# A gated causal convolution inside Strassen products: the weights, instead of the activations, stream through TensorE

## The chip, the cores and the metric

The kernel runs on one core of a Trainium2 chip. TensorE (PE) multiplies: it holds a 128x128 block of one operand (the stationary one, loaded by its own instruction, PEld) and streams columns of the other through it (the moving one) into a PSUM bank. VectorE (DVE) and ScalarE (ACT) work on tiles, GpSimd (POOL) here mainly issues DMAs, SyncE (SP) issues the other DMAs. The metric is the device time of one execution in microseconds (us), as the median of several runs.

## The reference

One hybrid block on 512 positions of width 1024: a normalised input is projected by a wide `w_in`; one branch is a short gated convolution, the other a chunked mLSTM; both are projected back and merged by gates, followed by two smaller projections. The part that matters here is the convolution branch, in float32:

```python
hn = rmsnorm(x, g_mix[l])
proj = jnp.einsum('bsd,de->bse', hn, w_in[l])
(xa, ba, ca, za, q, k, v, o, zb, ig, fg, ga, gb) = jnp.split(proj, SPLIT_POINTS, axis=-1)
# y[s] = w[0] u[s-2] + w[1] u[s-1] + w[2] u[s], with u = 0 before the start
ya = ba * causal_short_conv(ca * xa, conv_w[l], conv_b[l])
ya = jnp.einsum('bsc,cd->bsd', ya * jax.nn.silu(za), w_a_out[l])
```

`silu(z)` is z * sigmoid(z). `xa`, `ba`, `ca` and `za` are 512 x 1024 each. The convolution runs along the positions, separately for each channel, and `w_a_out` then contracts over the channels.

## The kernel before, in words

Every float32 product is made of three TensorE matmuls on a high and a low part (`mm3`, L234 to L236: high x high, low x high, high x low). The parts of the activations (`hn_hi`, `hn_lo`, and sums of them in `hs`) are made early; those of the weights are made as the weights arrive. A weight operand is a tile of 4 blocks of 128 rows by 512 columns (`wraw`); `split_half` makes its parts in two halves of 128x1024 elements: the high part `whi` on ACT (L181), the low part `wlo` on DVE (L182). Each has two buffers.

The order on PE, ACT, DVE and POOL is the order in which the program is written (a manual schedule), and each engine works strictly in it. After each stretch of matmuls the program calls `step`, and `step` calls `tick`, which writes down the work of the other engines for this stretch, in this order: the new tasks that the stretch before left in `fresh` (snaps of PSUM banks and what follows), one `split_half` of the operand that comes next, and then one more piece of every task in `active` and of those begun earlier (a task is a generator; a `yield` ends its piece).

Four times, for the channels 128c to 128c + 255 with c = 0, 2, 4, 6 (a pair of 128-channel blocks each, called first to fourth pair below), `strassen` computes one 512 x 1024 piece of the projection, the 256 columns each of x, c, b and z, as seven products instead of eight. Product j uses weight operand j; some operands are sums of two blocks of weights, made in place by accumulating DMAs that POOL issues (L157), or by DVE (L186). A product has two steps i = 0, 1, so a pair has 14 ticks, and the two halves of the next operand are split at the two ticks of the product before. The tasks `t1` to `t6` snap the banks into `s` and `v` (L347, on ACT) and add or subtract them (`out`, L351, on DVE). The four finished quarters go to `sink(n, t, ...)`: n = 0 is the x and c part, n = 1 the b and z part.

Before, the pairs run with the last argument of `strassen` true: the weights are stationary and 256 positions of activations move, so that the results come out with channels on the partitions and positions along them, one half of the positions at a time. `sink_conv` sorts its quarters to `first` to `fourth`: product of x and c into `cu`, three taps for each channel block into `cv`, gate by b, z and its sigmoid `cz`, and `put` writes the high part of the result to one tile named `ya` on ACT (L409) and the low part to another on DVE (L411). The block behind the pairs multiplies by `w_a_out` and reads `ya` as its moving operand, 512 positions wide.

Much later, in the tail, `lefts_3` prepares operands of a last set of Strassen products; `cut` (L241 on ACT, L242 on DVE) makes the high and low part of one of them, a tile named `ls`.

Of the kernel before, what the change touches and what calls it, by code (L numbers as in the profile page):

```python
# [9 lines left out]
F32 = mybir.dt.float32  # L10
# [4 lines left out]
P = 128  # L15
# [21 lines left out]
def hybrid_block(ctx, tc, x, p, g_mix, w_in, conv_w, conv_b, w_a_out, b_gates, g_head,  # L37
# [352 lines left out]
    def sink_conv(c, u, v, ya, ct):  # L390
# [4 lines left out]
        part = [slice(f * H2, (f + 1) * H2) for f in range(2)]  # L395
        held = {}

        def taps(f):
            to = v[:, part[f]]
            dve.tensor_scalar(to, u[:, f, 2:], w[f][2], None, ALU.mult)  # L400
            for j in range(2):
                dve.scalar_tensor_tensor(to, u[:, f, j:j + H2], w[f][j], to, ALU.mult, ALU.add)

        def put(src, h):
            if not ya:
                ya.extend(hp.tile([P, KT, S], F32R, name=f"ya{i}", tag=t, align_bytes=256) for i, t in enumerate(("qk", "vv")))
            to = [t[:, c:c + 2, h * H2:(h + 1) * H2] for t in ya]
            src = src.rearrange("p (f s) -> p f s", f=2)
            act.activation(to[0], src, AF.Copy)  # L409
            yield  # L410
            dve.tensor_tensor(to[1], src, to[0].bitcast(F32), ALU.subtract)  # L411

        def split(t):
            return t.rearrange("p (f s) -> p f s", f=2)

        def first(i, src):
            if i == 0:
                held["x"] = src
                return
            dve.memset(u[:, :, :2], 0.0)  # L420
            dve.tensor_tensor(u[:, :, 2:], split(held["x"]), split(src), ALU.mult)
            for f in range(2):
                yield
                taps(f)

        def second(i, src):
            if i == 0:
                for f in range(2):
                    dve.scalar_tensor_tensor(v[:, part[f]], v[:, part[f]], b[f], src[:, part[f]], ALU.add, ALU.mult)
                return  # L430
            z = temp("e", "cz")
            act.activation(z, src, AF.Sigmoid)
            dve.tensor_tensor(v, v, src, ALU.mult)
            yield
            dve.tensor_tensor(v, v, z, ALU.mult)
            yield
            yield from put(v, 0)

        def third(i, src):
            if i == 0:  # L440
                held["b"] = src
                return
            z = temp("e", "cz")
            act.activation(z, src, AF.Sigmoid)
            g = held["g"] = ct[0]
            dve.tensor_tensor(g, held["b"], src, ALU.mult)
            yield
            dve.tensor_tensor(g, g, z, ALU.mult)

        def fourth(i, src):  # L450
            if i == 0:
                held["x"] = ct[1]
                act.activation(held["x"], src, AF.Copy)
                yield
                return
            dve.tensor_copy(u[:, :, :2], u[:, :, H2:])
            dve.tensor_tensor(u[:, :, 2:], split(held["x"]), split(src), ALU.mult)
            g = held["g"]
            for f in range(2):
                yield  # L460
                taps(f)
            yield
            for f in range(2):
                dve.scalar_tensor_tensor(g[:, part[f]], v[:, part[f]], b[f], g[:, part[f]], ALU.add, ALU.mult)
            yield
            yield from put(g, 1)

        def sink(n, t, src):
            yield from ((first, fourth), (second, third))[n][t // 2](t % 2, src)
# [1074 lines left out]
```

## Time and profile before

| | us |
|---|---|
| median of 3 runs | 838.02 |
| lowest, highest run | 837.71, 838.5 |
| the profiled execution | 837.85 |
| its span in the profile | 836.1 |
| PE busy | 826.2 |
| DVE busy | 681.8 |
| ACT busy | 531.1 |
| POOL busy | 210.3 |

The span is the stretch that the trace covers, and 1.75 us of the execution lie around it. Busy times overlap, so each is read against the span, not added up. In the rows of a timeline stand start, duration, engine, line, operation, the tile written, an arrow, and the tiles read; in brackets the engine's idle time ahead of the row, and what ended it. PE's durations include its pipeline, so that consecutive matmuls overlap, and the time that one costs is the distance between starts. In the rows of windows stands, for each engine, its busy time and the number of instructions.

### The profile page before, as it was taken

The page shows a single profiled execution, that of the slowest core. Times are in us where ns is not written, and L with a number is a line of the kernel's source. Part 1 is how long each engine was busy: PE and PEld are TensorE (multiplying, and loading weights), DVE is VectorE, ACT ScalarE, POOL GpSimd, SP SyncE. Part 2 cuts the span into 40 slices and gives each one's busy share as a digit, 9 for nine tenths or more (in the row PEclk, how much of TensorE's full clock was granted, in tenths as well). Part 3 has the DMA queues.
Part 4 walks back from the last instruction along what each step waited for, and adds up shares of the span by engine and source line. Part 5 has one row for each costly group of instructions (what it writes and reads, how often), then busy time and mean ns, then how long its engine had stood idle before and what let it go on. Part 6 is the DMA issues. An engine that isn't in the chain of part 4 may idle for free.

```text
span 836.1 us, 12130 instructions
## 1 busy us (share of the span) xinstructions
PE 826.2 (99%) x4521; PEld 720.9 (86%) x4521; DVE 681.8 (82%) x944; ACT 531.1 (64%) x790; POOL 210.3 (25%) x212
## 2 busy tenths in 40 slices
PE   9999999999999999999999999999999999999995
PEld 7888888888889988888888999999998888888885
DVE  6688768998888777889878999797885779999565
ACT  6567665778665866577876484545448357757643
POOL 4203122213125221320322434242410212121031
PEclk9999999999999999999999999999999999999999
DMA  9748789769869897995997789999989698799402
GB/s 314 270 149 183 151 222 221 206 205 264 212 142 190 223 228 176 255 214 154 263 233 187 154 179 235 181 181 182 185 271 378 135 250 205 191 270 238 170 1 101
DMA packets 102947, 170.74 MB, mean 204 GB/s; under 512 B 5664, under 2 KB 47700, under 8 KB 102120
## 3 DMA queue, kind: packets, MB, share of 16 engines
q0 software_dynamic: 39136, 69.28, 44.0%
q1 hardware_dynamic: 59968, 94.64, 34.5%
q10 hardware_dynamic: 3784, 6.04, 2.2%
q8 instruction: 35, 0.57, 0.3%
q14 instruction: 24, 0.20, 0.1%
HBM read 153.16 MB, written 16.79 MB: 203 GB/s over the span
## 4 chain that ended last, share of the span: by engine, by line
PE 93%; DVE 5%; issue 1%; ACT 1%; POOLq 0%; POOL 0%; ACTq 0%; DVEq 0%
PE mm L235 28%; PE mm L234 28%; PE mm L236 28%; DVE wlo L182 2%; PE pv L234 1%; PE pv L236 1%; PE pv L235 1%; PE mm L590 1%; PE mmp L590 1%; PE sc L236 1%; PE sc L235 1%; PE sc L234 1%; PE ptp L491 0%; PE ptk L1329 0%; DVE xr L1353 0%
## 5 line engine op out<-in xcount | busy, mean ns | idle before, releaser
L182 DVE TENSOR_TENSOR wlo<-wraw,whi 128x1024 fp32r<-128x1024 f32 x245 | 300.7, 1228 | 81.3 <-ACT whi L181 75.0
L181 ACT ACTIVATE whi<-wraw 128x1024 fp32r<-128x1024 f32 x246 | 257.9, 1054 | 80.2 <-PE mm L236 38.0
L157 POOL DMA_DIRECT2D wraw<-in_w_in x106 | 129.3, 1390 | 296.0 <-DVE wlo L182 212.3
L347 ACT ACTIVATE s<-mm 128x512 f32<-128x512 f32 x84 | 50.2, 598 | 78.4 <-PE mm L236 77.2
L235 PE MATMUL mm<-wlo,hs 128*128 128x512 f32 x256 | 99.8, 390 | 0.0
L234 PE MATMUL mm<-whi,hs 128*128 128x512 f32 x256 | 99.7, 389 | 0.0
L236 PE MATMUL mm<-whi,hs 128*128 128x512 f32 x256 | 99.7, 389 | 0.0
L234 PE MATMUL mm<-hn_hi,whi 128*128 128x256 f32 (+1 forms) x304 | 93.3, 307 | 0.0
L236 PE MATMUL mm<-hn_hi,wlo 128*128 128x256 f32 (+1 forms) x304 | 93.0, 306 | 0.0
L235 PE MATMUL mm<-hn_lo,whi 128*128 128x256 f32 (+1 forms) x304 | 92.9, 305 | 0.0
L234 PE MATMUL mm<-hs,whi 128*128 128x256 f32 x320 | 90.6, 283 | 0.0
L235 PE MATMUL mm<-hs,whi 128*128 128x256 f32 x320 | 90.6, 283 | 0.0
L236 PE MATMUL mm<-hs,wlo 128*128 128x256 f32 x320 | 90.6, 283 | 0.0
L234 PE MATMUL mm<-whi,hn_hi 128*128 128x512 f32 x192 | 74.7, 389 | 0.0
L235 PE MATMUL mm<-wlo,hn_hi 128*128 128x512 f32 x192 | 74.7, 389 | 0.0
L236 PE MATMUL mm<-whi,hn_lo 128*128 128x512 f32 x192 | 74.7, 389 | 0.0
L234 PEld LDWEIGHTS mm<-hs,whi 128*128 128x128 f32 x320 | 61.4, 192 | 0.0
L235 PEld LDWEIGHTS mm<-hs,whi 128*128 128x128 f32 x320 | 61.4, 192 | 0.0
L236 PEld LDWEIGHTS mm<-hs,wlo 128*128 128x128 f32 x320 | 61.4, 192 | 0.0
L234 PEld LDWEIGHTS mm<-hn_hi,whi 128*128 128x128 f32 x304 | 58.1, 191 | 2.8 <-DVE hn_lo L245 0.4
L236 PEld LDWEIGHTS mm<-hn_hi,wlo 128*128 128x128 f32 x304 | 58.1, 191 | 2.6
L235 PEld LDWEIGHTS mm<-hn_lo,whi 128*128 128x128 f32 x304 | 58.1, 191 | 2.4
(342 smaller groups left out, 1724.6 us busy)
## 6 DMA issues: line engine op xcount, KB each, us to landing
wraw<-in_w_in SPq DMA_DIRECT2D x32, 1024.0 KB, 6.0
wraw<-in_w_in SPq DMA_DIRECT2D x46, 512.0 KB, 5.0
wraw<-in_w_in POOLq DMA_DIRECT2D x46, 512.0 KB, 7.4
wraw<-in_w_in POOLq DMA_DIRECT2D x60, 256.0 KB, 5.9
wraw<-in_w_b_out SPq DMA_DIRECT2D x7, 1024.0 KB, 6.9
wraw<-in_w_b_out POOLq DMA_DIRECT2D x12, 512.0 KB, 6.8
wraw<-in_w_o SPq DMA_DIRECT2D x5, 1024.0 KB, 6.2
wraw<-in_w_a_out SPq DMA_DIRECT2D x4, 1024.0 KB, 5.1
```

The source lines that it names most:

```text
L157: nc.gpsimd.dma_start(raws[to][:, ks, cs], src[:, ks, :], accum_op=ALU.add)
L181: act.activation(hi, t, AF.Copy)
L182: (e_lo or dve).tensor_tensor(lo, t, hi.bitcast(F32), ALU.subtract)
L234: pe.matmul(ps, lhsT=a[0], rhs=b[0], start=first, stop=False, **kw)
L235: pe.matmul(ps, lhsT=a[0], rhs=b[1], start=False, stop=False, **kw)
L236: pe.matmul(ps, lhsT=a[1], rhs=b[0], start=False, stop=last, **kw)
L347: act.activation(to[i], src, AF.Copy, scale=scale)
L590: pe.matmul(pss[n, t], lhsT=pT[u][:, k, t * P:(t + 1) * P], rhs=(whi, wlo)[v][2 * n + k], start=(k, i) == (0, 0), stop=(k, i) == (1, 2))
```

## The change

The four pairs now run with activations stationary (a block of 128 channels of the input by 128 positions) and the 512 columns of a weight operand moving, as other products of this kernel do: 24 matmuls of 512 columns a product in place of 48 of 256. The results then have positions on the partitions and channels along them, while the convolution and the next product need channels on the partitions. So:

- x * c is written to `u`, a quarter of `m` (L461). PE transposes it by 8 matmuls with the identity (`turned`, L403) into two PSUM banks `ptu`; ACT copies them with the last tap's weight and the bias (L426), and DVE adds the two other taps from PSUM (L409, `taps`).
- b and z go to a new tile `zb` (`place`), where b * z * sigmoid(z) is made (L468 to L471). For the first three pairs DVE transposes it in blocks of 32x32 (L474) and ACT moves the blocks into place in 16 instructions on 32 partitions each (L445), two in a tick. For the last pair PE transposes `zb`, by 8 more matmuls right behind those for `u`.
- `gated` multiplies both on DVE (L412) and writes the high part of `ya` on ACT (L413); `rest` writes the low part on DVE (L416).
- All this is the task `after`, which runs in the ticks of the next pair, starting one tick in (two after the first pair); the last pair's runs in the block of `w_a_out`.
- In the tail, the two parts of `ls` are made a step apart: the low part one step later than before.

```diff
@@ -387,86 +387,91 @@
         product(6, acc, None, lambda i: sink(0, 2 + i, acc[i]))
         order.reverse()
 
-    def sink_conv(c, u, v, ya, ct):
+    def sink_conv(c, zb, ya, last):
 
 
         w = [[cw[:, j * KT + c + f:j * KT + c + f + 1] for j in range(3)] for f in range(2)]
         b = [cb[:, c + f:c + f + 1] for f in range(2)]
-        part = [slice(f * H2, (f + 1) * H2) for f in range(2)]
-        held = {}
-
-        def taps(f):
-            to = v[:, part[f]]
-            dve.tensor_scalar(to, u[:, f, 2:], w[f][2], None, ALU.mult)
-            for j in range(2):
-                dve.scalar_tensor_tensor(to, u[:, f, j:j + H2], w[f][j], to, ALU.mult, ALU.add)
-
-        def put(src, h):
+        u, blocks = (m[:, i, :].rearrange("p (t f) -> p t f", t=NT) for i in (2, 3))
+        g, v = (m[:, i, :].rearrange("p (f s) -> p f s", f=2) for i in range(2))
+        gs = [g[:, f, :] for f in range(2)]
+
+        def turned(src):
+            pts = [ps_x.tile([P, S], F32, name="ptu", tag="x") for _ in range(2)]
+            for f in range(2):
+                for t in range(NT):
+                    pe.transpose(pts[f][:, t * P:(t + 1) * P], src[:, t, f * P:(f + 1) * P], ident)
+            return pts
+
+        def taps(f, pt):
+            for j in (1, 0):
+                to = v[:, f, 2 - j:]
+                dve.scalar_tensor_tensor(to, pt[:, :S - 2 + j], w[f][j], to, ALU.mult, ALU.add)
+
+        def gated(f):
+            dve.tensor_tensor(v[:, f, :], v[:, f, :], gs[f], ALU.mult)
+            act.activation(ya[0][:, c + f, :], v[:, f, :], AF.Copy)
+
+        def rest(f):
+            dve.tensor_tensor(ya[1][:, c + f, :], v[:, f, :], ya[0][:, c + f, :].bitcast(F32), ALU.subtract)
+
+        def after():
+            for _ in range(0 if last else 2 if c == 0 else 1):
+                yield
+            pts = turned(u)
+            if last:
+                gs[:] = turned(zb)
+            yield
+            for f in range(2):
+                act.activation(v[:, f, :], pts[f], AF.Identity, scale=w[f][2], bias=b[f])
+            yield
             if not ya:
                 ya.extend(hp.tile([P, KT, S], F32R, name=f"ya{i}", tag=t, align_bytes=256) for i, t in enumerate(("qk", "vv")))
-            to = [t[:, c:c + 2, h * H2:(h + 1) * H2] for t in ya]
-            src = src.rearrange("p (f s) -> p f s", f=2)
-            act.activation(to[0], src, AF.Copy)
-            yield
-            dve.tensor_tensor(to[1], src, to[0].bitcast(F32), ALU.subtract)
-
-        def split(t):
-            return t.rearrange("p (f s) -> p f s", f=2)
-
-        def first(i, src):
-            if i == 0:
-                held["x"] = src
+            if last:
+                for f in range(2):
+                    taps(f, pts[f])
+                    gated(f)
+                yield
+                for f in range(2):
+                    rest(f)
                 return
-            dve.memset(u[:, :, :2], 0.0)
-            dve.tensor_tensor(u[:, :, 2:], split(held["x"]), split(src), ALU.mult)
-            for f in range(2):
-                yield
-                taps(f)
-
-        def second(i, src):
-            if i == 0:
-                for f in range(2):
-                    dve.scalar_tensor_tensor(v[:, part[f]], v[:, part[f]], b[f], src[:, part[f]], ALU.add, ALU.mult)
-                return
-            z = temp("e", "cz")
-            act.activation(z, src, AF.Sigmoid)
-            dve.tensor_tensor(v, v, src, ALU.mult)
-            yield
-            dve.tensor_tensor(v, v, z, ALU.mult)
-            yield
-            yield from put(v, 0)
-
-        def third(i, src):
-            if i == 0:
-                held["b"] = src
-                return
-            z = temp("e", "cz")
-            act.activation(z, src, AF.Sigmoid)
-            g = held["g"] = ct[0]
-            dve.tensor_tensor(g, held["b"], src, ALU.mult)
-            yield
-            dve.tensor_tensor(g, g, z, ALU.mult)
-
-        def fourth(i, src):
-            if i == 0:
-                held["x"] = ct[1]
-                act.activation(held["x"], src, AF.Copy)
-                yield
-                return
-            dve.tensor_copy(u[:, :, :2], u[:, :, H2:])
-            dve.tensor_tensor(u[:, :, 2:], split(held["x"]), split(src), ALU.mult)
-            g = held["g"]
-            for f in range(2):
-                yield
-                taps(f)
-            yield
-            for f in range(2):
-                dve.scalar_tensor_tensor(g[:, part[f]], v[:, part[f]], b[f], g[:, part[f]], ALU.add, ALU.mult)
-            yield
-            yield from put(g, 1)
+            for i in range((P // B) ** 2):
+                if i % 2 == 0:
+                    if i < 4:
+                        taps(i // 2, pts[i // 2])
+                k, q = divmod(i, P // B)
+                src = blocks[k * B:(k + 1) * B].rearrange("p t (f q a) -> p t f q a", q=P // B, a=B)[:, :, :, q]
+                dst = g[q * B:(q + 1) * B].rearrange("p f (t b a) -> p t f b a", t=NT, a=B)[:, :, :, k]
+                act.activation(dst, src, AF.Copy)
+                if i % 2:
+                    yield
+            gated(0)
+            yield
+            rest(0)
+            gated(1)
+            yield
+            rest(1)
 
         def sink(n, t, src):
-            yield from ((first, fourth), (second, third))[n][t // 2](t % 2, src)
+            if n == 0:
+                x = src[:, :H2]
+                if t > 1:
+                    x = temp("e", "cx")[:, :H2]
+                    act.activation(x, src[:, :H2], AF.Copy)
+                dve.tensor_tensor(u[:, t, :], x, src[:, H2:], ALU.mult)
+                if t == NT - 1:
+                    active.append(after())
+                yield
+            elif t % 2:
+                bs, zs = (zb[:, t - 1:t + 1, i * H2:(i + 1) * H2] for i in range(2))
+                z = temp("e", "cz").rearrange("p (t f) -> p t f", t=2)
+                act.activation(z, zs, AF.Sigmoid)
+                dve.tensor_tensor(bs, bs, zs, ALU.mult)
+                yield
+                dve.tensor_tensor(bs, bs, z, ALU.mult)
+                if not last:
+                    yield
+                    dve.transpose(blocks[:, t - 1:t + 1, :], bs)
         return sink
 
     start_ctx, sp = open_pool("start")
@@ -1075,11 +1080,9 @@
     mp_ctx, mp = open_pool("merge")
     m = mp.tile([P, NT, D], F32, name="m", tag="m")
     cv_ctx, cvp = open_pool("conv")
-    cu = cvp.tile([P, 2, H2 + 2], F32, name="cu")
-    cv = cvp.tile([P, S], F32, name="cv")
-    ct = [m[:, 2 + i, CW:] for i in range(2)]
+    zb = cvp.tile([P, NT, S], F32, name="zb")
     for c in range(0, KT, 2):
-        strassen(hn_lhs, sink_conv(c, cu, cv, ya, ct), True)
+        strassen(hn_lhs, sink_conv(c, zb, ya, c == KT - 2), place=lambda n, t: zb[:, t, :] if n else temp("c"))
     close(hs_ctx, hn_ctx)
 
 
@@ -1257,8 +1260,9 @@
         for ks, pt in q:
             dve.tensor_tensor(f1[:, ks, :], f1[:, ks, :], pt, ALU.subtract)
         yield
-        cut(*o_s4, f1)
-        yield
+        act.activation(o_s4[0], f1, AF.Copy)
+        yield
+        dve.tensor_tensor(o_s4[1], f1, o_s4[0].bitcast(F32), ALU.subtract)
         for ks, f in f11:
             dve.tensor_tensor(f21[:, ks, :], f.rearrange("p (f s) -> p f s", f=2), f21[:, ks, :], ALU.subtract)
         u = yfp.tile([P, 2, HC, H2], F32R, name="lc", tag="yf2", align_bytes=256)
```

On ACT, the end of the third pair (products 5 and 6, up to the split of the second half of the next pair's first operand; `s` is a snap of a bank, `cz` the sigmoid of z, `cx` a copy of x), before:

```order
L347 ACTIVATE s<-mm 128x512
L181 ACTIVATE whi_5626<-wraw_4798 128x1024
L432 ACTIVATE cz<-c 128x512
L347 ACTIVATE s<-mm 128x512
L181 ACTIVATE whi_5664<-wraw_5285 128x1024
L453 ACTIVATE m<-mm 128x512
L181 ACTIVATE whi_5696<-wraw_5285 128x1024
L409 ACTIVATE ya_4726<-cv 128x2x256
L444 ACTIVATE cz<-c 128x512
L181 ACTIVATE whi_5733<-wraw_5427 128x1024
```

and now:

```order
L347 ACTIVATE s<-mm 128x512
L181 ACTIVATE whi_5166<-wraw_4593 128x1024
L413 ACTIVATE ya_4673<-m 128x512
L468 ACTIVATE cz<-zb 128x512
L347 ACTIVATE s<-mm 128x512
L181 ACTIVATE whi_5193<-wraw_4933 128x1024
L413 ACTIVATE ya_4673<-m 128x512
L460 ACTIVATE cx<-mm 128x256
L181 ACTIVATE whi_5218<-wraw_4933 128x1024
```

The copies of `ya` that ACT made behind the last split of that stretch now stand twice between two splits, once ahead of `cz` and a snap, once ahead of `cx`; they belong to the pair before.

On DVE, the same place, before:

```order
L351 TENSOR_TENSOR c<-s,v 128x512
L182 TENSOR_TENSOR wlo_5627<-wraw_4798,whi_5626 128x1024
L433 TENSOR_TENSOR cv<-cv,c 128x512
L351 TENSOR_TENSOR c<-s,v 128x512
L182 TENSOR_TENSOR wlo_5665<-wraw_5285,whi_5664 128x1024
L435 TENSOR_TENSOR cv<-cv,cz 128x512
L182 TENSOR_TENSOR wlo_5697<-wraw_5285,whi_5696 128x1024
L446 TENSOR_TENSOR m<-c 128x512
L456 COPY cu<-cu 128x2x2
L457 TENSOR_TENSOR cu<-m,mm 128x2x256
L182 TENSOR_TENSOR wlo_5734<-wraw_5427,whi_5733 128x1024
L411 TENSOR_TENSOR ya_4727<-cv,ya_4726 128x2x256
L448 TENSOR_TENSOR m<-m,cz 128x512
```

and now (L412 and L416 are the gated product and the low part of `ya`; `m` holds `u`, the taps' result and the gate):

```order
L351 TENSOR_TENSOR zb<-s,v 128x512
L182 TENSOR_TENSOR wlo_5167<-wraw_4593,whi_5166 128x1024
L412 TENSOR_TENSOR m<-m 128x512
L469 TENSOR_TENSOR zb<-zb 128x2x256
L351 TENSOR_TENSOR zb<-s,v 128x512
L182 TENSOR_TENSOR wlo_5194<-wraw_4933,whi_5193 128x1024
L416 TENSOR_TENSOR ya_4674<-m,ya_4673 128x512
L412 TENSOR_TENSOR m<-m 128x512
L471 TENSOR_TENSOR zb<-zb,cz 128x2x256
L461 TENSOR_TENSOR m<-cx,mm 128x256
L182 TENSOR_TENSOR wlo_5219<-wraw_4933,whi_5218 128x1024
```

Two products L412, on which the two `ya` of ACT wait, and one low part L416 have come in among the low parts of the weights; the product that reads `cx` now stands ahead of the last of these.

On PE, the block behind the pairs, where its first step ends and its second begins (`whi` and `wlo` with the higher numbers are the second half of its first operand), before:

```order
L236 MATMUL mm<-whi_6175,ya_4727 128x512
L234 MATMUL mm<-whi_6175,ya_4726 128x512
L235 MATMUL mm<-wlo_6176,ya_4726 128x512
L236 MATMUL mm<-whi_6175,ya_4727 128x512
L234 MATMUL mm<-whi_6145,ya_4726 128x512
L235 MATMUL mm<-wlo_6146,ya_4726 128x512
```

and now:

```order
L234 MATMUL mm<-whi_5548,ya_4673 128x512
L235 MATMUL mm<-wlo_5549,ya_4673 128x512
L236 MATMUL mm<-whi_5548,ya_4674 128x512
L403 MATMUL ptu<-ident,m 128x128 x8
L403 MATMUL ptu<-ident,zb 128x128 x8
L234 MATMUL mm<-whi_5525,ya_4673 128x512
L235 MATMUL mm<-wlo_5526,ya_4673 128x512
```

16 transposes stand between the two steps, and the second 8 read `zb`.

On DVE in the tail, where `ls` is cut (`xr` is the residual stream), before:

```order
L1353 TENSOR_TENSOR xr<-xr,mm 128x512
L182 TENSOR_TENSOR wlo_7285<-wraw_6991,whi_7284 128x1024
L242 TENSOR_TENSOR ls<-yf_6193,ls 128x1024
L1353 TENSOR_TENSOR xr<-xr,mmb 128x512
L182 TENSOR_TENSOR wlo_7306<-wraw_6991,whi_7305 128x1024
L1263 TENSOR_TENSOR yf_6193<-f_7150,yf_6193 128x512
L1263 TENSOR_TENSOR yf_6193<-f_7152,yf_6193 128x512
```

and now:

```order
L1357 TENSOR_TENSOR xr<-xr,mm 128x512
L182 TENSOR_TENSOR wlo_6680<-wraw_6386,whi_6679 128x1024
L1357 TENSOR_TENSOR xr<-xr,mmb 128x512
L182 TENSOR_TENSOR wlo_6700<-wraw_6386,whi_6699 128x1024
L1265 TENSOR_TENSOR ls<-yf_5566,ls 128x1024
L1267 TENSOR_TENSOR yf_5566<-f_6545,yf_5566 128x512
L1267 TENSOR_TENSOR yf_5566<-f_6547,yf_5566 128x512
```

The low part of `ls` has moved behind an addition to `xr` and the low part of a half of weights.

More of the change, by code (lines that the diff above doesn't have):

```diff
@@ L439, in third @@
-        def third(i, src):
-            if i == 0:
-                held["b"] = src
-                return
-            z = temp("e", "cz")
-            act.activation(z, src, AF.Sigmoid)
-            g = held["g"] = ct[0]
-            dve.tensor_tensor(g, held["b"], src, ALU.mult)
-            yield
-            dve.tensor_tensor(g, g, z, ALU.mult)
-        def fourth(i, src):
-            if i == 0:
-                held["x"] = ct[1]
-                act.activation(held["x"], src, AF.Copy)
-                yield
-                return
-            dve.tensor_copy(u[:, :, :2], u[:, :, H2:])
-            dve.tensor_tensor(u[:, :, 2:], split(held["x"]), split(src), ALU.mult)
-            g = held["g"]
-            for f in range(2):
-                yield
-                taps(f)
-            yield
-            for f in range(2):
-                dve.scalar_tensor_tensor(g[:, part[f]], v[:, part[f]], b[f], g[:, part[f]], ALU.add, ALU.mult)
-            yield
-            yield from put(g, 1)
@@ L468, in sink @@
-        def sink(n, t, src):
-            yield from ((first, fourth), (second, third))[n][t // 2](t % 2, src)
+            if last:
[5 more added lines that the diff above has]
+                    rest(f)
+                return
+            for i in range((P // B) ** 2):
[8 more added lines that the diff above has]
+                    yield
@@ new lines, in after, with sink @@
+            gated(0)
+            yield
+            rest(0)
+            gated(1)
+            yield
+            rest(1)
+        def sink(n, t, src):
+            if n == 0:
[6 more added lines that the diff above has]
+                    active.append(after())
+                yield
+            elif t % 2:
[3 more added lines that the diff above has]
+                dve.tensor_tensor(bs, bs, zs, ALU.mult)
+                yield
+                dve.tensor_tensor(bs, bs, z, ALU.mult)
+                if not last:
+                    yield
+                    dve.transpose(blocks[:, t - 1:t + 1, :], bs)
```

## The prediction

> **What bounds the kernel now.** I read the page's first part and its chain first, then the windows of the convolution, then single rows of the timeline where the change puts something.
>
> ```profile
> span 836.1 us, 12130 instructions
> PE 826.2 (99%) x4521; PEld 720.9 (86%) x4521; DVE 681.8 (82%) x944; ACT 531.1 (64%) x790; POOL 210.3 (25%) x212
> PE 93%; DVE 5%; issue 1%; ACT 1%; POOLq 0%; POOL 0%; ACTq 0%; DVEq 0%
> ```
>
> TensorE (PE) is busy 99% of the span and carries 93% of the chain that ended last, so the kernel gets faster only by fewer or cheaper matmuls or by one of the few stalls going. In turn any wait that the change brings to PE is paid in full. Next the windows: first pair, all four pairs, and the matmuls of a product with 512 columns moving, just ahead of them.
>
> ```profile
> core 0: us, PE busy (x) PEld busy (x) DVE busy (x) ACT busy (x) POOL busy (x), PEclk, DMA share, GB/s
> 457.20:497.50 40.30, 40.30 (x337) 40.27 (x336) 35.97 (x52) 25.98 (x35) 12.86 (x11) 1.00 0.79 168
> 457.20:618.40 161.20, 161.20 (x1344) 161.15 (x1343) 139.99 (x198) 92.00 (x120) 56.42 (x47) 1.00 0.90 188
> 439.78:457.00 17.22, 17.22 (x77) 14.26 (x76) 15.62 (x31) 12.18 (x20) 4.89 (x4) 1.00 0.71 182
> ```
>
> The four pairs hold 1344 matmuls of 256 columns in 161.20 us, back to back at a granted clock of 1.00: 0.1199 us each. With 512 columns 76 take 17.22 us, 0.2266 each, less than two of the small ones (0.2399). In the first pair, the fullest, VectorE (DVE) has work for 35.97 of 40.30 us and ScalarE (ACT) for 25.98: both have room, but not much on DVE.
>
> The prediction rests on how PE, ACT and DVE hand over to each other, so here are the rows of one such handover and of the end of the convolution.
>
> ```profile
> 604.06 0.28 PE L236 MATMUL mm<-hs,wlo 128*128 128x256 f32 x1
> 604.18 0.28 PE L234 MATMUL mm<-hs,whi 128*128 128x256 f32 x1
> ...
> 604.38 0.60 ACT L347 ACTIVATE s<-mm 128x512 f32<-128x512 f32 x1 [2.61 <-PE mm L236]
> 604.87 1.05 ACT L181 ACTIVATE whi<-wraw 128x1024 fp32r<-128x1024 f32 x1
> ...
> 605.95 1.23 DVE L182 TENSOR_TENSOR wlo<-wraw,whi 128x1024 fp32r<-128x1024 f32 x1 [0.26 <-ACT whi L181]
> ...
> 617.34 0.62 ACT L409 ACTIVATE ya<-cv 128x512 fp32r<-128x512 f32 x1
> 617.86 0.62 ACT L444 ACTIVATE cz<-c 128x512 f32<-128x512 f32 x1
> 618.38 1.05 ACT L181 ACTIVATE whi<-wraw 128x1024 fp32r<-128x1024 f32 x1
> ...
> 617.47 1.23 DVE L182 TENSOR_TENSOR wlo<-wraw,whi 128x1024 fp32r<-128x1024 f32 x1 [0.99 <-ACT whi L181]
> ...
> 620.09 1.22 DVE L182 TENSOR_TENSOR wlo<-wraw,whi 128x1024 fp32r<-128x1024 f32 x1
> 621.23 0.68 DVE L411 TENSOR_TENSOR ya<-cv,ya 128x512 fp32r<-128x512 f32 x1
> 621.83 0.69 DVE L448 TENSOR_TENSOR m<-m,cz 128x512 f32<-128x512 f32 x1
> ```
>
> Start to start: a PE group's end (604.18) to the snap `s` 0.20; snap to the weights' high part `whi` 0.49; `whi` to its low part `wlo` 1.08; `wlo` to the next on DVE 1.14; a 512-column operation 0.60 on DVE and 0.52 on ACT. A 512-column DVE operation ends 0.69 after its start, and with 0.03 of handover its reader on ACT starts 0.72 after it.
>
> **The change part by part.** *Wider matmuls.* 672 of 512 columns take the place of 1344: 672 x 0.2267 = 152.34, so **-8.86**. [...]
>
> *Transposes on PE.* 8 for each of three pairs and 16 in a row for the last. The nearest group in the trace, which also reads a tile `m` and sits between matmuls:
>
> ```profile
> 724.46 0.40 PE L236 MATMUL mm<-whi,l 128*128 128x512 f32 x1
> 724.69 1.04 PE L1211 MATMUL pth<-ident,m 128*128 128x128 f32 x8
> 725.48 0.48 PE L234 MATMUL mm<-whi,l 128*128 128x512 f32 x1
> 725.80 0.39 PE L235 MATMUL mm<-wlo,l 128*128 128x512 f32 x1
> ```
>
> 8 push the next matmul back by 0.79, and that one takes 0.32 to the next instead of 0.23: 0.88 a group. 3 x 0.88 + (2 x 0.79 + 0.09) = **+4.31**. Should the transposes fall where PE waits for weights anyhow, they would cost less than this; apart from the wait for `zb`, none of the waits below lies at that tick, so I take the row.
>
> *The low part in the tail.*
>
> ```profile
> 758.92 0.39 PE L234 MATMUL mm<-whi,lb 128*128 128x512 f32 x1
> 759.61 0.50 PE L235 MATMUL mm<-wlo,lb 128*128 128x512 f32 x1 [0.30 <-DVE wlo L182]
> 759.94 0.40 PE L236 MATMUL mm<-whi,lb 128*128 128x512 f32 x1
> ...
> 756.60 1.22 DVE L242 TENSOR_TENSOR ls<-yf,ls 128x1024 fp32r<-128x1024 f32 x1
> 757.74 0.68 DVE L1353 TENSOR_TENSOR xr<-xr,mmb 128x512 f32<-128x512 f32 x1
> 758.34 1.22 DVE L182 TENSOR_TENSOR wlo<-wraw,whi 128x1024 fp32r<-128x1024 f32 x1
> ```
>
> PE waits here for the `wlo` of 758.34: 758.92 to 759.94 is 1.02 where two matmuls take 0.45, so 0.57 is lost. The change puts `ls` (1.14) behind this `wlo`, which is then ready 1.14 earlier, more than the stall. **-0.57**; the bounds are -0.57 and 0 (were the wait for a transfer). `ls` itself comes a `wlo` later, and later still stands `yf` L1263 that waits for nothing of it.
>
> *Work on DVE and ACT.* Nearest rows, grouped by form:
>
> ```profile
> L1339 ACT ACTIVATE yf<-ptk,prm 128x256 f32<-128x256 f32 x12 | 4.7, 472 | 1.0 <-PE ptk L1329 1.0
> L827 ACT ACTIVATE yc<-yc 32x256 f32<-32x256 f32 x40 | 16.5, 414 | 0.7
> L818 DVE STREAM_TRANSPOSE yc<-gty 128x512 f32<-128x512 f32 x16 | 11.2, 702 | 0.0
> ```
>
> A pair's new ACT work is 16 block moves (0.41), two scaled copies and two `ya` (0.6 each), two `cx` (0.47): 9.9 us, and it drops the old `ya` and copies; DVE gets two block transposes (0.70 each) and four wide taps where it had twelve narrow ones. Either engine stays below the 39 us that PE now needs for a pair, so the totals fit and I cost them at nothing. The order is another matter: ACT and DVE work strictly in their order, and a `ya` on ACT that waits for its product on DVE holds up every `whi` behind it.
>
> *The end of a pair, by hand.* Zero is the start of product 6; its first half ends at 2.72, its second at 5.44, and PE reads the second half of the next operand's weights from 6.80 (`whi`) and 7.03 (`wlo`): 5.44 + 6 and 7 matmuls. With the order shown above for the third pair's end:
> ACT snap -2.52 (the product's first half ended at -2.72), `whi` -2.03; DVE `wlo` -0.95, then at 0.20 the gated product L412; ACT `ya` 0.92, `cz` 1.44, second snap 1.96 (its matmuls were ready at 0.20), `whi` 2.45; DVE `wlo` 3.53, low part L416 4.68, second L412 5.28; ACT `ya` 6.00, `cx` 6.52, and only then, with 0.37 for `cx`, `whi` of the second half 6.89; DVE `wlo` 7.97 to 9.20. PE wanted it at 7.03: 2.17, and 0.1 for the restart: **2.3 lost**. In the kernel before this `whi` waits only for product 6's first half and is done well ahead (`wlo` at 617.47, where PE is through with the pair at 618.58). What PE loses here, ACT and DVE do not get back: the waits are theirs.
> The last pair's end has the same order: **2.3** again. There the 8 transposes of `zb` follow too. They need L471, which stands behind the next `wlo`: 9.12 + L416 0.60 + L469 0.60 + L461 0.4 + `wlo` 1.14 + L471 0.69 = 12.55, while PE, at 9.2 + 5 matmuls + 8 transposes, is there at 11.4: **1.1**.
> At the second pair's end the gated part is a tick later, since the first pair's `after` has one yield more. Nothing holds `whi` of the second half; but DVE and ACT are late in the next product: second `ya` 8.08, `cz` 8.60, `cx` 9.12, `whi` 9.49, `wlo` 10.57 to 11.72 (just in time), then L416, L471 and L474 ahead of the second `wlo`, which ends at 14.15. PE, with 0.88 of transposes between, wants it at 13.35: **0.8**. At the first pair's end nothing of an earlier pair is left, and the margin is 1.4: nothing. Sum of waits **+6.5**; bounds 0 (if the moves and `ya` run shorter than their rows) and 10, by the POOL rival below.
>
> *DMA.* The weight additions on POOL are the same in number and order. SP's loads for the block after the convolution now stand between loads of `sg_d`, which wait for temps; I get that weight's landing within 0.2 us of when ACT comes to it, so nothing.
>
> Sum against the profiled execution (837.85, of which 836.1 is the span): 837.85 - 8.86 + 4.31 - 0.57 + 6.5 = 839.2. The median of the runs, 838.02, lies 0.17 above it: **839.4 us**. A change of 0.2% (1.7 us) is what a measurement here can tell from none.
>
> **The rivals.** *The waits are hidden.* Then the sum is 838.02 - 8.86 + 4.31 - 0.57 = 832.9. For it speaks that both engines have room on the whole; against it that the two `ya` at each end both stand between a DVE product and the next `whi`, and that 2.17 of lateness needs four operations to be off by half a microsecond. Half hidden gives 834.5 to 837.3.
>
> *POOL's additions land late (slower).* Each sum of two weight blocks has to land before `whi` can read it.
>
> ```profile
> 518.80 2.43 POOL L157 DMA_DIRECT2D wraw<-in_w_in  x2 [6.38 <-DVE cv L400]
> wraw<-in_w_in POOLq DMA_DIRECT2D x60, 256.0 KB, 5.9
> wraw<-in_w_in POOLq DMA_DIRECT2D x3, 256.0 KB, 7.8
> ```
>
> They take 5.9 as a rule and 7.8 in the second pair (the middle of three around 521 us), and are issued only when `whi` and `wlo` of the old contents are made. Every product now lasts 5.44 instead of 5.76 (48 x 0.1199), and counting back from there the last addition, for product 6's second half, has about 7.1 us until it is wanted. At 5.9 it costs nothing. At 7.8 it is 0.7 late; if all pairs do as the second did, that is 0.7 at two ends, and at the second pair's end, whose first half had only 0.14 to spare (11.72 against 11.99 less the restart), the whole lateness of that chain comes through, some 1.8. 0.7 + 0.7 + 1.8 = 3.2, and the time is 842.6. It decides above 7.1.
>
> *The transposes cost more than their row.* They read tiles written shortly before. If each took as long as a 512-column matmul with its restart (0.32), 40 would take 12.8 instead of 4.31: 847.9. Against it is the row of 8 in 0.79. [...]
>
> **How the numbers follow.** Forecast 839.4, own range 837.5 to 841.2: 0.61, half of it beyond 839.7 (slower) and half within 0.2%. Hidden waits 0.18 (faster). Half hidden 0.07, of which 0.05 faster. Late additions 0.12, dear transposes 0.02 (slower). So faster 0.23, same 0.33, slower 0.44. The range that leaves out less than 2 in 10 goes from the hidden case to the late additions, 832.3 to 842.6.
>
> **What would show it.** In the windows of the pairs: 672 matmuls in about 152.4 us and 24 transposes in about 2.6. PE rows that wait for `wlo` L182 of about 2.2 us 1.4 us into the fourth pair and into the block behind it, with ACT's `ya` L413 named as idle before `cx`; a 0.8 us wait in the second product of the third pair; a wait of `ptu` for `zb` L471 of 1.1. No wait for `wlo` at the `lb` matmuls of the tail. If the `whi` behind `cx` starts before 4.7 on the clock above, or if PE shows no idle rows there, the forecast is wrong and the hidden case holds; if `whi` waits for POOL's transfers, the late case.

## The result

The changed kernel takes 843.86 us (median of 6 runs, 842.41 to 846.49) where the kernel before takes 837.96 (837.71 to 838.5): a ratio of 1.0071, interval 1.0055 to 1.0087. It is slower by 5.9 us. The forecast was 839.4, the range ended at 842.6; both were too low. The profiled execution is the shortest of the six, 842.41, and lies 1.45 below the median; before, the two lie 0.11 apart (0.17 with the three runs that the prediction had). Both the miss and the 1.45 need an explanation.

The page of the changed kernel, as it was shown of before:

```profile
span 840.6 us, 10885 instructions
PE 825.1 (98%) x3889; PEld 689.4 (82%) x3889; DVE 675.7 (80%) x910; ACT 557.0 (66%) x850; POOL 210.3 (25%) x212
PE 88%; DVE 4%; ACT 3%; DMA 2%; issue 1%; POOL 0%; POOLq 0%; ACTq 0%; SPq 0%; DVEq 0%
```

PE's share of the chain that ended last fell from 93% to 88%, ACT's rose from 1% to 3%, and DMA (2%) came into it: the chain now leaves PE several times. The list of what PE waited for (us in total, times, longest) names it; of before it had 0.3 for `wlo` and nothing for `whi`:

```profile
PE mm L235 <- DVE wlo L182: 3.9, 6, 0.8
PE mm L234 <- ACT whi L181: 1.8, 2, 0.9
PE ptu L403 <- DVE zb L471: 0.8, 1, 0.8
```

Now the end of the third pair, ACT first, DVE behind it, then PE:

```profile
573.10 0.63 ACT L413 ACTIVATE ya<-m 128x512 fp32r<-128x512 f32 x1 [1.89 <-DVE m L412]
573.63 0.62 ACT L468 ACTIVATE cz<-zb 128x512 f32<-128x512 f32 x1
574.15 0.58 ACT L347 ACTIVATE s<-mm 128x512 f32<-128x512 f32 x1
574.63 1.05 ACT L181 ACTIVATE whi<-wraw 128x1024 fp32r<-128x1024 f32 x1
578.17 0.63 ACT L413 ACTIVATE ya<-m 128x512 fp32r<-128x512 f32 x1 [2.50 <-DVE m L412]
578.71 0.37 ACT L460 ACTIVATE cx<-mm 128x256 f32<-128x256 f32 x1
578.98 1.05 ACT L181 ACTIVATE whi<-wraw 128x1024 fp32r<-128x1024 f32 x1
...
575.71 1.23 DVE L182 TENSOR_TENSOR wlo<-wraw,whi 128x1024 fp32r<-128x1024 f32 x1 [0.26 <-ACT whi L181]
576.86 0.68 DVE L416 TENSOR_TENSOR ya<-m,ya 128x512 fp32r<-128x512 f32 x1
577.46 0.68 DVE L412 TENSOR_TENSOR m<-m 128x512 f32<-128x512 f32 x1
580.05 1.23 DVE L182 TENSOR_TENSOR wlo<-wraw,whi 128x1024 fp32r<-128x1024 f32 x1 [0.52 <-ACT whi L181]
...
578.77 0.39 PE L236 MATMUL mm<-whi,hn_lo 128*128 128x512 f32 x1
580.08 0.50 PE L234 MATMUL mm<-whi,hn_hi 128*128 128x512 f32 x1 [0.92 <-ACT whi L181]
581.34 0.50 PE L235 MATMUL mm<-wlo,hn_hi 128*128 128x512 f32 x1 [0.76 <-DVE wlo L182]
```

Twice ACT stands idle at `ya` until DVE has made the gated product, 1.89 and 2.50 us, while the next `whi` stands behind it. PE loses (580.08 - 578.77 - 0.23) + (581.34 - 580.08 - 0.23) = 2.11, and 0.11 at the next matmul: 2.2 where the prediction said 2.3. (The 0.11 is the restart: the first matmul behind each of these waits lasts 0.50 where the others last 0.39.) At the end of the fourth pair it is 2.2 again (1.8 and 1.5 in the list are those two places), and the wait for `zb` is 0.9 with its restart (forecast 1.1).

What the prediction does not have stands in the second pair:

```profile
514.19 0.39 PE L234 MATMUL mm<-whi,hs 128*128 128x512 f32 x1
515.08 0.50 PE L235 MATMUL mm<-wlo,hs 128*128 128x512 f32 x1 [0.51 <-DVE wlo L182]
...
531.37 0.39 PE L234 MATMUL mm<-whi,hn_hi 128*128 128x512 f32 x1
532.34 0.50 PE L235 MATMUL mm<-wlo,hn_hi 128*128 128x512 f32 x1 [0.59 <-DVE wlo L182]
...
537.78 0.49 PE L234 MATMUL mm<-whi,hn_hi 128*128 128x512 f32 x1
539.04 0.50 PE L235 MATMUL mm<-wlo,hn_hi 128*128 128x512 f32 x1 [0.77 <-DVE wlo L182]
```

With the restarts 0.8, 0.9 and 1.2: 2.9 together. The first two are within the second pair, the third is at its end. They lead back to other rows, of ACT, DVE, POOL and ACT again:

```profile
507.32 1.45 ACT L426 ACTIVATE m<-ptu,prm 128x512 f32<-128x512 f32 x2 [2.65 <-DMA yt_d<-m]
...
512.03 1.53 DVE L409 SCALAR_TENSOR_TENSOR m<-ptu,prm,m 128x511 f32<-128x511 f32 x2
513.48 0.41 DVE L461 TENSOR_TENSOR m<-c 128x256 f32<-128x256 f32 x1
513.81 1.22 DVE L182 TENSOR_TENSOR wlo<-wraw,whi 128x1024 fp32r<-128x1024 f32 x1
...
516.08 1.52 DVE L409 SCALAR_TENSOR_TENSOR m<-ptu,prm,m 128x511 f32<-128x511 f32 x2
517.52 0.41 DVE L461 TENSOR_TENSOR m<-c 128x256 f32<-128x256 f32 x1
517.86 3.49 DVE L182 TENSOR_TENSOR wlo<-wraw,whi 128x1024 fp32r<-128x1024 f32 x3
...
519.37 4.90 POOL L157 DMA_DIRECT2D wraw<-in_w_in  x4 [10.07 <-DVE wlo L182]
...
529.97 1.06 ACT L181 ACTIVATE whi<-wraw 128x1024 fp32r<-128x1024 f32 x1 [1.26 <-DMA wraw<-in_w_in]
...
535.88 0.63 ACT L413 ACTIVATE ya<-m 128x512 fp32r<-128x512 f32 x1 [1.89 <-DVE m L412]
536.42 0.37 ACT L460 ACTIVATE cx<-mm 128x256 f32<-128x256 f32 x1
536.68 1.05 ACT L181 ACTIVATE whi<-wraw 128x1024 fp32r<-128x1024 f32 x1
```

ACT's copy of the turned `u` overwrites the half of `m` from which the last head's result is being stored to DRAM, and waits 2.65 for the store. The taps need this copy and stand ahead of `wlo` on DVE. The two at 512.03 delay the `wlo` of 513.81, for which PE waits at 514 us; the two at 516.08 delay the three `wlo` behind them, and with these POOL's additions of weights are issued late. The split of 529.97 then waits 1.26 for weights to land, which becomes PE's wait at 531. The wait at 538 is again an end of a pair: ACT is idle for 1.89 us at `ya` (535.88), ahead of the `whi` of 536.68.

The rows sum up: 837.85 - 8.86 + 4.31 - 0.57 + 6.5 (the waits that were forecast: 2.22 and 2.21 at the two ends, 0.93 for `zb`, 0.84 in the third pair's second product, and two of 0.14 shortly ahead of the ends) + 2.9 + 0.25 (a wait for a PSUM bank in the first pair) = 842.4, where the profiled execution took 842.41.

### The profile page after: what moved, and what is told of

It reads as the page before. It is cut to its first block, busy times and chain, and to the rows that moved or that the text cites. A ratio compares the mean times of both kernels' runs of the same rounds, so it can differ in the third digit from the quotient of the medians.

```text
span 840.6 us, 10885 instructions
## 1 busy us (share of the span) xinstructions
PE 825.1 (98%) x3889; PEld 689.4 (82%) x3889; DVE 675.7 (80%) x910; ACT 557.0 (66%) x850; POOL 210.3 (25%) x212
## 4 chain that ended last, share of the span: by engine, by line
PE 88%; DVE 4%; ACT 3%; DMA 2%; issue 1%; POOL 0%; POOLq 0%; ACTq 0%; SPq 0%; DVEq 0%
PE mm L235 26%; PE mm L236 26%; PE mm L234 26%; DVE wlo L182 2%; DMA wraw<-in_w_in 2%; ACT whi L181 1%; PE pv L234 1%; PE pv L236 1%; PE pv L235 1%; DMA yt_d<-m 1%; PE mm L595 1%; PE mmp L595 1%; PE sc L236 1%; PE sc L235 1%; PE sc L234 1%
## 5 line engine op out<-in xcount | busy, mean ns | idle before, releaser
L235 PE MATMUL mm<-wlo,hs 128*128 128x512 f32 x384 | 149.7, 390 | 0.5 <-DVE wlo L182 0.5
L234 PE MATMUL mm<-whi,hs 128*128 128x512 f32 x384 | 149.6, 389 | 0.0
L236 PE MATMUL mm<-whi,hs 128*128 128x512 f32 x384 | 149.5, 389 | 0.0
L235 PEld LDWEIGHTS mm<-wlo,hs 128*128 128x128 f32 x384 | 72.1, 188 | 15.6 <-DVE wlo L182 0.9
L236 PEld LDWEIGHTS mm<-whi,hs 128*128 128x128 f32 x384 | 72.1, 188 | 15.1
L234 PEld LDWEIGHTS mm<-whi,hs 128*128 128x128 f32 x384 | 72.1, 188 | 15.0 <-ACT whi L181 0.4
L235 PEld LDWEIGHTS mm<-wlo,hn_hi 128*128 128x128 f32 x288 | 54.1, 188 | 15.1 <-DVE wlo L182 4.1
L234 PEld LDWEIGHTS mm<-whi,hn_hi 128*128 128x128 f32 x288 | 54.1, 188 | 13.2 <-ACT whi L181 1.7
L236 PEld LDWEIGHTS mm<-whi,hn_lo 128*128 128x128 f32 x288 | 54.1, 188 | 11.2
L234 PE MATMUL mm<-whi,l 128*128 128x512 f32 x112 | 43.8, 391 | 0.0
L235 PE MATMUL mm<-wlo,l 128*128 128x512 f32 x112 | 43.7, 390 | 0.0
L236 PE MATMUL mm<-whi,l 128*128 128x512 f32 x112 | 43.6, 389 | 0.0
L234 PE MATMUL mm<-hn_hi,whi 128*128 128x512 f32 (+1 forms) x112 | 39.0, 348 | 0.0
```

The costliest lines, as they stand in the source:

```text
L234: pe.matmul(ps, lhsT=a[0], rhs=b[0], start=first, stop=False, **kw)
L235: pe.matmul(ps, lhsT=a[0], rhs=b[1], start=False, stop=False, **kw)
L236: pe.matmul(ps, lhsT=a[1], rhs=b[0], start=False, stop=last, **kw)
```

## The experiments

Three theories were told apart: *order* (ACT, held at `ya`, holds the splits), *store* (the wait for the last head's store), and *landing* (the added weights come late by themselves). Each kernel's time is a median beside the kernel before on the same chip.

**tail_only**: `cut(*o_s4, f1)` split into two steps in the kernel before, as in the change, and nothing else.

> The kernel before with the tail's edit alone: the low part of ls one step later, the pairs as they were. If the wait of TensorE at 758.92 was for the low part of the weights behind ls, it goes: 0.57 us, 837.4, and no row at the lb matmuls waits. If it was for something else (a transfer), the wait moves to another row and the time stays at 838.0. If ls is now late for the product that reads it, a wait at the matmuls on ls appears and the time is above 838.

837.42 against 838.00 (ratio 0.9997, interval 0.9988 to 1.0006). The medians differ by 0.58 as expected, but the interval of the ratio contains 1, so that the times alone don't show it. The trace does: no wait for `wlo` is left anywhere, and none for `ls`. The stretch of the program behind the last matmul on `ya` is 165.05 us long, 165.60 before: 0.55.

**ya_later**: in the first three pairs' tasks the copies of `ya` stand a tick after their product, and the first low part a tick later too (for the last pair `high(f)` follows `gated(f)` at once, so that nothing moves there).

```diff
             dve.tensor_tensor(v[:, f, :], v[:, f, :], gs[f], ALU.mult)
+
+        def high(f):
             act.activation(ya[0][:, c + f, :], v[:, f, :], AF.Copy)
...
             gated(0)
             yield
+            high(0)
+            gated(1)
+            yield
+            high(1)
             rest(0)
-            gated(1)
             yield
             rest(1)
```

> The changed kernel with one thing moved: the two copies of ya on ScalarE come one tick after the gated products on VectorE that they read (and the first low part one tick later too), so that ScalarE no longer waits for VectorE ahead of a split of weights. Order theory: the two waits at the ends of the third and fourth pair (2.2 us each) go, the wait of the transposes for zb falls from 0.9 to 0.1, and the 0.8 at the second product of the third pair goes, 6 in all: 837 to 838 against 843.9. Rival, the transfers: the splits there wait for sums of weights that land late, the copies only fill the time until then; the waits stay, 843 to 844. The waits within the second pair (514 us, 531 us, 538 us) should stay by both.

836.66 (0.998, 0.9971 to 0.9989): 7.2 less than the changed kernel, a little faster than the kernel before, and below the 837 to 838 expected. Both waits of 2.2 are gone from the trace, and so is the one in the third pair; the transposes of `zb` still wait 0.5 (0.8 in the changed kernel), where 0.1 was expected. For these waits the order theory holds and the rival falls. In the second pair the first two waits stayed and grew (1.3 at 515 us, 1.6 at 533); of the third, at the pair's end, 0.1 is left, which neither theory had. From the last matmul ahead of the pairs on, the profiled execution is 5.6 shorter than that of the changed kernel, and the waits account for that; the other 1.6 of the 7.2 are taken up at after_again.

**no_war**: the last head's store reads `hn_hi` instead of `m`.

> The changed kernel with the last head's store to DRAM reading another tile of the same size instead of m (so what it stores is not that head's result); traffic and order stay. Store theory: ScalarE's copy of the transposed u (L426) in the second pair had to wait 2.65 us until the store had read m, and this delay runs on through the pair: without it the wait at 514 us (0.8) goes, and if the late landing at 531 and 538 us is a consequence, those 2.1 too: 840.5 to 843. Rival: the additions of weights land late by themselves, because the DMA engines are 93% busy in this pair: only 0.8 goes, the waits at 531 and 538 us stay, 843. The waits at the ends of the third and fourth pair stay at 2.2 by both.

842.45 (1.0053, 1.0040 to 1.0067), profiled 841.56. The waits at 514 and 531 us are gone, 1.6 of the 2.9; that at 538 stayed at 1.1. So the store was behind the first two. The store theory had hoped for the third as well; the rival had that at 531 stay too.

**no_adds**: no accumulating DMAs in the four pairs.

> The changed kernel without the accumulating DMAs on GpSimd in the four pairs: the operands there stay unsummed blocks, so the convolution's numbers are others. Everything that waits for a landing sum goes, and a quarter of the traffic. Order theory: the 2.2 at the ends of the third and fourth pair and the 0.8 in the third pair stay, since ScalarE waits for VectorE there; the waits at 531 and 538 us (2.1) go; 841 to 842. Rival, the transfers are behind the end waits too: all go, 834 to 836. If the runs then spread as little as the kernel before (0.8 us instead of 4), the spread of the changed kernel comes from the landings.

841.83 (1.0046, 1.0032 to 1.0059). The 2.2 at both ends and the 0.8 stayed though no sum was left to land: the additions have no part in them. The waits at 514 and 531 went, and of the one at 538 0.3 is left. The time did not fall by as much as the waits; the reason is given at after_again.

**later_321, later_taps, later_321_taps**: on top of ya_later, the task's start moved (a), the taps moved (b), or both. The letters in the diff are added here.

```diff
-            for _ in range(0 if last else 2 if c == 0 else 1):
+            for _ in range(0 if last else 3 - c // 2):          # (a)
-                    if i < 4:
-                        taps(i // 2, pts[i // 2])
+                    if 8 <= i < 12:                              # (b)
+                        taps(i // 2 - 4, pts[i // 2 - 4])
```

> As ya_later (836.7), and the task that follows a pair starts three, two, one ticks in after the first, second and third pair (two, one, one there), so that ScalarE's copy of u meets the last head's store when it has read m. Store theory: the wait in the second pair's middle (1.3 us at 515 in ya_later) goes, and since weights are then split sooner, the sums are issued sooner and some of the 1.6 at 533 us goes too: 834.5 to 835.5. Rival, late landings by themselves: only the first goes, 835.4, or the copy just moves into the next tight place, 836.7.

> As ya_later, and the four taps on VectorE come four ticks later, so that they no longer stand ahead of the low parts after which GpSimd issues the additions of product 4 to 6. Order theory: those additions are issued about 1.5 us sooner, and the waits at 533 us (1.6 with its restart) fall to 0.3 or less: 835.0 to 835.5. Rival, busy DMA engines: they are issued sooner but land at the same time as before, 836.7. The wait for the store (1.3 at 515) stays by both.

> Both of the moves together. If they are independent, 836.7 less 1.3 less 1.3: 833.5 to 834.5, near the sum without any wait of the prediction (832.9). If the late start and the late taps push the gated products into the next pair's tight first ticks, waits appear there and it is no better than the better of the two, 835.0 to 835.5.

834.71 (0.9959, 0.9946 to 0.9971), 833.68 (0.9948, 0.9934 to 0.9962) and 833.64 (0.9947, 0.9935 to 0.996). The moves are not independent: the taps alone take away every wait in the second pair. In later_taps ACT still waits for the store, 2.84 us where it was 2.65 in the changed kernel, and POOL's additions come 2.4 earlier than there, though the pairs begin 0.3 later (ACT, then POOL):

```profile
507.75 1.45 ACT L428 ACTIVATE m<-ptu,prm 128x512 f32<-128x512 f32 x2 [2.84 <-DMA yt_d<-m]
...
516.92 4.90 POOL L157 DMA_DIRECT2D wraw<-in_w_in  x4 [7.31 <-DVE wlo L182]
```

The store therefore cost nothing by itself. What cost was that the taps, which need the copy, stood on DVE ahead of the low parts of the weights; without them there the 2.84 us of ACT's lateness are hidden. The first two waits needed both, the store and the taps' place: no_war took away the one, later_taps the other. My expectation for later_taps, that PE's wait at 515 us would stay, was wrong, and so was its 835.0 to 835.5. From issue to landing those additions took 6.7 us in the changed kernel and 6.0 here, so the larger part of the gain is the earlier issue; in the kernel before, the prediction shows 7.8, and no wait came of it.

**bare**: no transposes on PE, taps, gated products or block moves; `ya` is made from x * c without a wait of ACT for DVE (the convolution is left out).

> The changed kernel without transposes, taps, gating and block moves: ya is made from x times c directly, with no wait of ScalarE for VectorE, so the convolution itself is left out. Matmul theory: with 672 matmuls of 512 columns for 1344 of 256 the time is 838.0 less 8.9 less 0.6, 828.5; with the 0.3 at the first pair and what landings cost in the second, 828.5 to 830. If the waits at the ends of the third and fourth pair came from the matmuls' greater speed alone (splits that can't keep up), they are still here: 833 to 834. If the wider matmuls gained less than the rows say (a gap that grows with the columns), 835 or more with no waits in the trace.

828.60 (0.9884, 0.9869 to 0.9899). From the last matmul of the head ahead of the pairs to the first that reads `ya` it is 152.83 us, before 161.58: -8.75, with 0.25 of waiting in it. The matmul term is right, and there is no wait at the pairs' ends, so the faster matmuls alone don't bring those.

**taps_only**: (b) alone, in the changed kernel.

> The changed kernel with the taps four ticks later, as in later_taps, but with the copies of ya where the change put them. If the taps are what delays the second pair, the waits at 514, 531 and 538 us go (2.8 in the profiled execution of the changed kernel), and the 2.2 at the ends of the third and fourth pair and the 0.8 after the second stay: the profiled execution near 839.5, and if the 1.4 by which the changed kernel's median lies above its profiled execution comes from landings in that pair too, the median is 839.5 as well; if it comes from something else, 841. If the copies of ya feed the waits of the second pair too, about 1 of the 2.8 stays.

841.78 (1.0046, 1.0034 to 1.0059). The waits at 514 and 531 us went and 0.3 of the third was left, so it is the taps' place in the changed kernel too. At the second pair's end ACT is still idle for 1.90 us at `ya`, but now PE loses only the 0.3: the third wait needs the late additions and the `ya` on ACT together, and ya_later, which left the additions late, took it away as well. Yet the profiled execution, 841.61, is only 0.8 shorter than that of the changed kernel. The expected 839.5 was missed for the reason that follows.

**after_again**: the changed kernel, profiled a second time.

> The changed kernel again, for a second profiled execution of it. If the waits of the second pair come from landings, they differ from the first one's 0.8, 0.9 and 1.2 in proportion to this execution's time, while the two at the ends (2.2, 2.2) and the one for zb (0.9) are the same to 0.1. If the times of this kernel spread for another reason (a granted clock that dips after a wait), matmuls 0.43 apart without a wait stand behind one of the waits.

844.87 (1.0081, 1.0067 to 1.0095), profiled 844.97. All waits are as in the first one to 0.1. Of the 2.6 by which it is longer, 0.5 lie ahead of the pairs and 0.5 in the tail; the rest stands behind the third pair's end (windows, then PE):

```profile
582.95:586.36 3.41, 3.41 (x10) 2.70 (x9) 3.41 (x6) 1.54 (x2) 1.54 (x2) 0.54 0.90 115
...
582.37 0.40 PE L234 MATMUL mm<-whi,hn_hi 128*128 128x512 f32 x1
582.61 0.54 PE L235 MATMUL mm<-wlo,hn_hi 128*128 128x512 f32 x1
582.95 0.63 PE L236 MATMUL mm<-whi,hn_lo 128*128 128x512 f32 x1
583.38 0.63 PE L234 MATMUL mm<-whi,hn_hi 128*128 128x512 f32 x1
583.81 0.63 PE L235 MATMUL mm<-wlo,hn_hi 128*128 128x512 f32 x1
```

For 3.4 us the granted clock is 0.54, and matmuls start 0.43 apart instead of 0.23: 8 x 0.20 = 1.6 us lost with nothing waited for. taps_only (0.54) and no_adds (0.53) show the same stretch at the same place, the first profiled execution (1.00 from 582.40 to 585.80 us) and no_war (a mean clock of 0.998, after_again 0.995) do not. ya_later (0.998) leaves out the wait ahead of this place and has no such stretch; that fits the 1.6 left over there, though only its one profiled execution shows it.

**held_before**: six copies that nobody reads ahead of one split in the kernel before, that of the fourth pair's first operand (`held_operand` is its number, `dummy` a tile that nothing else uses).

```diff
+        if h == 1 and i == held_operand:
+            for _ in range(6):
+                act.activation(dummy, hn_hi[:, 0, :].bitcast(F32), AF.Copy)
         act.activation(hi, t, AF.Copy)
```

> The kernel before with one thing added: ScalarE makes six copies of 128x512 that nobody reads (0.52 us each) ahead of the split that TensorE wants first in the second half of the fourth pair's first operand. By the rows of before that split has about 0.9 to spare, so TensorE waits 2.2 us there, once, as at the end of the changed kernel's third pair. If a wait of this size costs only itself, every execution takes 840.0 (837.8 and 2.2), spread as the kernel before. If TensorE's granted clock can fall to half behind such a wait, as in three of five profiled executions that had it, some executions take 841.6 to 841.8 and others 840, and a profiled one of the slower shows 3.4 us at a clock near 0.5 some 3 us behind the wait.

842.78 (1.0047, 1.0033 to 1.0061); single times 840.37, 841.55, 842.78, 842.86, 842.97. The copies took 0.65 each, more than the 0.52 expected, and PE lost 3.15 (2.03 + 0.10 + 0.92 + 0.10) in place of 2.2, so 841.1 was to be expected without more. The profiled execution, 842.78, has the stretch:

```profile
583.90:587.30 3.40, 3.40 (x19) 3.40 (x18) 2.90 (x4) 1.24 (x2) 1.82 (x2) 0.52 0.68 85
```

Here the clock of 0.52 follows a wait alone, in the kernel before, with none of the changed matmuls. The stretch is in four of the six traces that have a wait of 2 to 3 us at this place; before and bare, without such a wait, show 1.00 over the pairs (457 to 618 and 457 to 610 us). This is what can lie between the changed kernel's profiled execution and its median; the start of the program, whose last matmul ahead of the pairs starts at 457.0 to 458.5 us in these traces, can make up another part. Only the shortest of the six runs has a trace, so how the 1.45 divide is not shown.

**all_zb**: later_321_taps, and the last pair's `turned(zb)` behind the `yield`, one step after `turned(u)`.

> As later_321_taps (833.6), and the last pair's 8 transposes of zb one step after those of u. The wait for zb (0.5, with its restart 0.7) goes: 832.9 to 833.1, the prediction's sum with no wait. If the scaled copies and the taps, which now stand a step apart from the gate, delay the last low parts of ya instead, a wait for ya appears in the second half of that block and the time is 833.6 or more.

833.01 (0.9940, 0.9926 to 0.9953): the fastest, 4.8 us below the kernel before in the same comparison. The list of what PE waited for has neither `whi` nor `zb`, and 0.2 for `wlo`:

```profile
PE mm L235 <- DVE wlo L182: 0.2, 1, 0.2
```

## Why the prediction was wrong

- *Wider matmuls, -8.86; transposes, +4.31; tail, -0.57*: right. bare gives -8.75 for the pairs with 0.25 of waiting. By the medians all_zb less bare is 833.01 - 828.60 = 4.41; by the traces the pairs take 2.72 longer and the block behind them 1.80, 4.5 together, so the transposes were forecast a little low. The tail gave 0.55 to 0.58. all_zb, in which nearly no wait is left, is at the 832.9 that the prediction gave for hidden waits.
- *The end of a pair, by hand, 2.3 + 2.3 + 1.1 + 0.8*: right, in place, cause and size (2.2, 2.2, 0.9, 0.8). ya_later took them away by moving ACT's copies, all but 0.8 of the wait for `zb` with its restart, which all_zb took away. no_adds shows that the additions had no part in them.
- *"the totals fit and I cost them at nothing"* and *"At the first pair's end nothing of an earlier pair is left, and the margin is 1.4: nothing"*: the step that failed first. It went by the engines' totals and by what the pairs leave to each other at their ends, and looked neither at the order within a pair nor at what the last head still reads: `m`, for its store. The runs showed in its place that the taps, held up by the store, stood on DVE ahead of low parts of the weights, and that the additions which follow these were issued late: 0.8 and 0.9 us.
- *At the second pair's end, "Nothing holds `whi` of the second half"*: not so. A `ya` stands ahead of it, at which ACT is idle for 1.89 us. With the additions in time that costs 0.3 (taps_only, no_adds), with late ones 1.2. The three waits, 2.9 us, are again waits for an order.
- *The rival of late additions* had 1.8 at the second pair's end, where the waits at 531 and 538 us are 2.1, and its 842.6 is close to the profiled 842.41. That is luck in part: it put the lateness down to a landing of 7.8 instead of 5.9, in all pairs. Measured were 6.7, below the 7.1 that it needed; late was the issue. The 0.7 that it had at each of two other ends did not come.
- *The first pair*: 0.25 for a PSUM bank whose reader on DVE stands behind two products of the head. PE reached it earlier because its products are shorter. Not in the sum.
- *What a wait costs*: I priced a wait by its length and 0.1 for the restart. Where the clock fell behind it, to 0.54 in after_again, 1.6 came on top. I had carried over 0.17 from before as the distance between the profiled execution and the median, and it is 1.45. The clock and a start of the program that differs between runs are what the traces offer for it; that they make it up is argued, not shown.
- 839.4 + 2.9 + 0.25 + (1.45 - 0.17) = 843.8, measured 843.86. The range ended at one late-landing case and had no room for two misses of the same sign.

## What to carry to other kernels

Where engines work in a fixed order, read the queue and not the share: ACT was busy 66% of the span and still cost PE 5 us, because a copy that waits for DVE stood ahead of a split that PE needed. Put a handover between two engines a step apart, so that the second finds the first done, and move work that nobody waits for (here the taps) behind the work that feeds a DMA issue. When a buffer is used anew, look for its last reader among the DMAs too.

## What the runs showed of the hardware

A wait of TensorE of 2 to 3 us (2.2 with its restart in the changed kernel, 3.15 in held_before) was followed, about 1 us after it ended and in four of six traces, by 3.4 us at a granted clock of 0.52 to 0.54 (held_before 0.52, no_adds 0.53, after_again and taps_only 0.54). In after_again matmuls of 512 columns then started 0.43 us apart instead of 0.23. In the changed kernel the wait is in two parts, with a matmul between them. Why the same wait was followed by the lower clock in one execution of this kernel and not in another is not shown. At the end of the fourth pair, behind a wait of the same size, the clock was 1.00 both in the changed kernel's first profiled execution (621 to 631 us) and in after_again (622.25 to 632 us); why it did not fall there is open.
